# Layer 0 of a hybrid decoder trunk: the product of probabilities and values emitted one step later

## The chip, the cores and the metric

The kernel runs on one core of a Trainium2 chip. The metric is the device time of one execution in microseconds (us); the time of a kernel is the median of its runs. Its engines are named as in the profile: PE (TensorE, matrix products; PEld are its weight loads), DVE (VectorE), ACT (ScalarE), POOL (GpSimd) and SP (SyncE, which issues the transfers).

## The reference, cut to what matters

The input x is [1, 512, 1024] in float32. Two residual layers and a last norm follow one another; the change lies in layer 0:

```python
def even_layer(x, g_norm, w_in, b_f, w_out):
    z = rms_norm(x, g_norm) @ w_in             # [512, 8208]
    qa, ka, va, ga, fa, qb, kb, vb, gb = split(z)
    ya = forgetting_attention(qa, ka, va, log_sigmoid(fa + b_f))   # 16 heads x 64
    yb = dilated_attention(qb, kb, vb)                             # 16 heads x 64
    y = concatenate([ya * silu(ga), yb * silu(gb)])
    return x + y @ w_out
```

Both attentions are causal softmax attentions over 512 tokens. In forgetting attention the logit of query t and key s gets c_t - c_s, with c the running sum of the log forget gates. The dilated one is the mean, weighted by their denominators, of three dilated windows; the kernel folds it into one softmax with an added table. Layer 1 is chunkwise retention with a group norm, a gate and an output projection.

## The kernel before, in words

All matrix products run on numbers split into a high and a low part: `split(hi, lo, src)` rounds on ACT (line 132) and subtracts on DVE (line 134 or 136). A product of two split matrices takes three matmuls (`three`, lines 186 to 188). In the profile the line numbers of these helpers stand for many users, so the names of the tiles tell them apart: `pf` and `pt` are projections, `po` the output projection, `w_h` and `w_l` the split weights, `ka` and `kl` the high and low part of projected keys, `pth` and `ptl` those of the transposed probabilities, `yh` and `yl` those of the gated output.

The 32 heads of layer 0 go in 8 groups of 4, in the order dilated, four forgetting, three dilated. In stage n the attention of group n is emitted in 16 steps (4 heads times k = 0 to 3), and between the steps, in equal shares, the fillers: the gate projection of group n, the value projection of group n + 1, the output projection of an earlier group, and the key and query projections of group n + 1. The function `interleave` does that.

A step (hn, k) works on three heads at once. For head hn it emits the scores and the softmax of query block 3 - k (PE lines 442 and 443, DVE `pi` line 446, ACT exp line 448, DVE reciprocal line 449, POOL scaling line 450). For head hn - 1 it emits the transposes of key block k (PE line 457) and their split into `pth` (ACT) and `ptl` (DVE). Then come the products of the probabilities and values (`pv_block`): two matmuls per key block, with `pth` (line 469) and with `ptl` (line 470), summed up in the PSUM tile `ps_o`. After key block 3 `finish_head` reads `ps_o`: ACT copies one half to `tmp` (line 483), DVE adds the other to give `y` (line 484); after every second head POOL multiplies by the gate (line 486), and ACT and DVE split the result into `yh` and `yl`.

Buffers that the text comes back to: `ps_o` has one, `pth` and `ptl` have one for each key block, `kl` has one. `kl` and `ka` are the source of three transfers that SP issues (lines 396 to 398), so that the next `kl` can be written only after these have read the last:

```python
                kl = qp.tile([P, S], F32R, tag="kl", name="kl", bufs=1)
                split(ka, kl, ps)
                dma(out=r32(kb[64:128, :]), in_=r32(kl[64:128, :]))
                dma(out=r32(kb[0:64, :]), in_=r32(ka[64:128, :]))
                dma(out=r32(ka[64:128, :]), in_=r32(kl[0:64, :]))
```

A group's key projection gives two such `kl` (heads 0 and 1, heads 2 and 3).

What each engine executes in which order is not the order of emission itself: except in a part at the start that asks for its own order, the framework that builds the program orders the instructions of each engine, earlier emission first where several are ready by its own estimate of times. On the chip each engine then takes its list as it stands.

Of the kernel before, what the change touches and what calls it, by code (L numbers as in the profile page):

```python
# [14 lines left out]
P = 128  # L15
# [5 lines left out]
WARM = 12                     # matmuls that raise the tensor engine's clock  # L21
# layer 0: the order of the groups of 4 heads, dilated (D) and forgetting (F), and
# the groups whose output projection runs beside the attention of a group
# [3 lines left out]
OFF = (0, 128, 384, 768)      # column of query block i in a packed lower triangle  # L27
OFFT = (0, 512, 896, 1152)    # column of key block j in a packed transposed triangle
# [3 lines left out]
def _tables():  # L32
    """Constants that depend on the shapes alone."""
    p = np.arange(P)[:, None]
    g = np.arange(S)[None, :]
    ident = np.eye(P, dtype=np.float32)

    d = p - g + 384
    mult = ((d >= 0) & (d <= 128)).astype(np.int64)
    mult += (d >= 0) & (d % 4 == 0)  # L40
    mult += (d >= 0) & (d % 16 == 0)
    dil = np.where(mult > 0, -np.log(np.maximum(mult, 1).astype(np.float64)), MASKED).astype(np.float32)

    causal = np.where(np.arange(P)[None, :] <= p, 0.0, MASKED).astype(np.float32)

    half = 128
    inv = (np.float32(1.0) / (np.float32(10000.0) ** np.linspace(0.0, 1.0, half, dtype=np.float32))).astype(np.float32)
    ang = (np.arange(S, dtype=np.float32)[None, :] * inv[:, None]).astype(np.float32)
    rot = np.stack([np.cos(ang.astype(np.float64)), np.sin(ang.astype(np.float64))], axis=1).astype(np.float32)

    lg = np.log1p(-np.power(np.float32(2.0), np.float32(-5.0) - np.arange(4, dtype=np.float32))).astype(np.float32)
    rel = (g - p).astype(np.float64)
    dec = np.where(rel[:, None, :] >= 0,
                   np.exp(lg.astype(np.float64)[None, :, None] * np.maximum(rel, 0.0)[:, None, :]),
                   0.0) / 16.0
    return {"ident": ident, "dil": dil, "causal": causal, "rot": rot, "dec": dec.astype(np.float32)}
# [3 lines left out]
def trunk(ctx: ExitStack, tc, x, even_norm, even_w_in, even_b_f, even_w_out,  # L60
# [17 lines left out]
    xres = keep.tile([P, NT, D], F32, name="xres")  # L78
    xT = keep.tile([P, 2, KT, S], F32R, name="xT")     # normed x^T: high part, low part
# [4 lines left out]
    # the table of the first square roots, loaded beside the first transfers  # L84
# [9 lines left out]
    def rstd_of(v):  # L94
        """1 / sqrt(v) of a [128, 1] tile, refined by a Newton step."""
        sd = sm.tile([P, 1], F32, tag="sd", name="sd")
        act.activation(sd, v, AF.Sqrt)
        r = sm.tile([P, 1], F32, tag="rs", name="rs")
        dve.reciprocal(r, sd)
        e = sm.tile([P, 1], F32, tag="re", name="re")  # L100
        dve.scalar_tensor_tensor(e, r, v, r, ALU.mult, ALU.mult)
        dve.tensor_scalar(e, e, -0.5, 1.5, ALU.mult, ALU.add)
        dve.tensor_tensor(r, r, e, ALU.mult)
        return r

    def row_scale(t, junk):
        """1 / rms of the rows of token tile t of the residual; junk: a tile to write the squares to."""
        ss = sm.tile([P, 1], F32, tag="ss", name="ss")
        act.activation(junk, xres[:, t, :], AF.Square, accum_out=ss)
        v = sm.tile([P, 1], F32, tag="var", name="var")  # L110
        dve.tensor_scalar(v, ss, 1.0 / D, EPS, ALU.mult, ALU.add)
        return rstd_of(v)
# [3 lines left out]
    def half_stats(st, t, c, junk):  # L116
        """The same, from the two halves of the columns; the second gives 1 / rms."""
        ss = sm.tile([P, 1], F32, tag="ss", name="ss")
        act.activation(junk, xres[:, t, c * H:(c + 1) * H], AF.Square, accum_out=ss)
        v = sm.tile([P, 1], F32, tag="var", name="var")  # L120
        dve.tensor_scalar(v, ss, 1.0 / D, st["v"] if c else EPS, ALU.mult, ALU.add)
        st["v"] = v
        if c:
            st["r"] = rstd_of(v)

    def rms(t, gain, dst):
        """dst = rms_norm of token tile t of the residual."""
        dve.scalar_tensor_tensor(dst, xres[:, t, :], row_scale(t, dst), gain, ALU.mult, ALU.mult)

    def split(hi, lo, src, scale=1.0):  # L130
        """hi + lo = scale * src, each with 12 significant bits."""
        act.activation(hi, src, AF.Copy, scale=scale)  # L132
        if scale == 1.0:
            dve.tensor_tensor(lo, src, r32(hi), ALU.subtract)  # L134
        else:
            dve.scalar_tensor_tensor(lo, src, scale, r32(hi), ALU.mult, ALU.subtract)
# [11 lines left out]
    # a chunk is (DRAM [rows, cols], deinterleave); rows * cols = 512 * 256  # L148
# [41 lines left out]
    # Pieces of tensor engine work: a list of chunks and a generator that emits  # L190
    # the work and yields the time of the matmuls emitted since the last yield.
    def proj_features(w, c0, done, deinterleave=False):
        """done(b, PSUM [128 features, 512 tokens]) for the two halves of 256 columns of w."""
# [17 lines left out]
    def proj_tokens(w, c0, done, by_tile=False):  # L211
        """done(b, PSUM [128 tokens, 2 token tiles, 256 columns]) for the two pairs of token tiles.
        by_tile: one token tile after the other, as x^T comes."""
# [21 lines left out]
    def out_proj(y, w, rows, by_tile=None):  # L235
        """residual += y^T^T @ w; a chunk is 256 rows, from rows[i], of 512 columns;
        y(i): the high and low parts of two row tiles of y^T.
        by_tile: all of the weights held, the token tiles finished one after the other."""
        nc_, nk = len(rows), 2 * len(rows)
        # the chunk beyond the buffers of the stream has its own  # L240
# [30 lines left out]
    def interleave(steps, fillers, upto=None):  # L271
        """Emit the steps with the fillers' work between them: evenly, or the share upto[i]
        of it by the end of step i; the rest after the last step."""
# [14 lines left out]
    # =================== layer 0 ===================  # L288
# [17 lines left out]
    with ExitStack() as l0:  # L306
# [7 lines left out]
        bf = cst.tile([32, 1], F32, name="bf")              # for the products with the low part: 0  # L314
# [8 lines left out]
        c_th = cst.tile([P, NT, 16], F32, name="c_th")      # -c, [token, tile, head]  # L323
# [3 lines left out]
        def forget_gates():  # L327
            c_hs = ap_.tile([16, S], F32, tag="bias", name="c_hs", bufs=3)   # [head, token]
# [25 lines left out]
            dve.tensor_tensor(na, zz, nz, ALU.min)          # -|z|  # L354
            e = tl("f_e")
            act.activation(e, na, AF.Exp)                   # exp(-|z|)
            # log1p(e) = 2 atanh(s), s = e / (2 + e) <= 1/3
# [13 lines left out]
            # log_sigmoid = min(z, 0) - 2 pol  # L371
# [17 lines left out]
        def evac_k(store):  # L389
            def done(b, ps):  # L390
# [4 lines left out]
                # both heads [h; l]  # L395
# [6 lines left out]
        def evac_q(store):  # L402
            def done(b, ps):
                # both heads [h; l] and [l; h]
# [11 lines left out]
        def evac_v(store):  # L416
            def done(b, ps):
# [4 lines left out]
                # even heads [vh | vl], odd heads [vl | vh]  # L422
# [14 lines left out]
        def softmax_block(hs, i):  # L437
# [6 lines left out]
            st = sm.tile([P, 3], F32, tag="st", name="st", bufs=8)     # -max, sum, 1/sum  # L444
# [27 lines left out]
        def finish_head(hs):  # L472
            """O = high + low part; after a pair of heads: y = O * silu(g), split."""
# [15 lines left out]
        def fox_bias(head):  # L489
            """(c_s - c_t) and the causal mask, built two blocks ahead of their use."""  # L490
# [60 lines left out]
        order = []          # fillers of stage n, beside the attention of group n  # L551
# [14 lines left out]
        def step(hn, k):  # L566
            """Blocks of the bias two steps ahead, of the softmax of head hn, of P^T and P V of the heads before."""
            def go():
# [8 lines left out]
                if 0 <= hn - 1 < len(heads):  # L577
                    transpose_block(heads[hn - 1], k)
                    if k:
                        pv_block(heads[hn - 1], k - 1)  # L580
                if k == 0 and hn >= 2:
                    pv_block(heads[hn - 2], 3)
                    finish_head(heads[hn - 2])
            return go

        # the tensor engine's clock rises under load: keep it busy while x comes
# [31 lines left out]
        for n in range(8):  # L618
            steps = [step(hn, k) for hn in range(4 * n, 4 * n + 4) for k in range(4)]
            if n == 7:  # L620
                steps += [step(32, k) for k in range(4)] + [step(33, 0)]
# [4 lines left out]
    # =================== layer 1 ===================  # L626
    with ExitStack() as l1:
# [10 lines left out]
        def rotate_done(r, which):  # L638
            """[128 frequencies, 2 parities, 512 tokens], rotated and split."""
# [109 lines left out]
        # the last head: its output projection follows the token tiles  # L749
# [40 lines left out]
```

## Time and profile before

| | us |
|---|---|
| median of 3 runs | 1036.57 |
| lowest and highest run | 1035.21, 1036.67 |
| span of the profiled execution, first to last instruction | 1035.3 |
| PE busy | 1002.6 |
| DVE busy | 637.0 |
| ACT busy | 472.4 |
| POOL busy | 247.4 |

The page of the profile gives a span for the profiled execution and no time of its own beside it; the median of the runs is 1.3 us longer than this span. Busy shares are of the span. In a timeline the first two columns are the start from the span's start and the duration, both in us, and a bracket holds the idle time of the engine before the instruction and what ended it. `L470` is line 470 of the kernel. Ends of matmuls are modelled by the profiler, starts are recorded.

### The profile page before, as it was taken

Reading aid. Unit: us, or ns where it says so; the run is one execution under the profiler, and the core shown is the slowest. Engines: PE = TensorE matmul, PEld = TensorE weight load, DVE = VectorE, ACT = ScalarE, POOL = GpSimd, SP = SyncE. Lnnn points to the kernel's source line nnn. Section 1 sums busy time; section 2 is a strip of 40 time slices with the busy share of each in tenths; the row PEclk is TensorE's granted clock in tenths of the full one; section 3 lists DMA queues with packets and bytes.
Section 4 is the critical chain, followed back from the end, with each engine's and each line's share of the span. In section 5 each row is a group of like instructions: output and inputs, shape, how many; then the busy total and the mean of one; then the engine's idle time right before and its main releaser. Section 6 shows DMA issues by size and latency. Waiting matters only on the chain.

```text
span 1035.3 us, 15756 instructions
## 1 busy us (share of the span) xinstructions
PE 1002.6 (97%) x5836; PEld 869.6 (84%) x5836; DVE 637.0 (62%) x1389; ACT 472.4 (46%) x987; POOL 247.4 (24%) x326
## 2 busy tenths in 40 slices
PE   5999999999999999999999989999999999999997
PEld 5879788888887888987887769978998899889975
DVE  6465676575584576675657684377645744674476
ACT  5345464464554545644657473333323232333233
POOL 3011354454354352211212140023100300030012
PEclk8999999999999999999999999999999999999999
DMA  7554878635647776437454125321222222312112
GB/s 211 133 134 90 150 100 103 177 77 120 156 90 108 143 84 139 107 79 145 76 130 123 41 62 184 102 79 64 82 82 91 72 82 82 102 61 95 69 41 82
DMA packets 84444, 107.42 MB, mean 104 GB/s; under 512 B 6016, under 2 KB 63616, under 8 KB 84240
## 3 DMA queue, kind: packets, MB, share of 16 engines
q1 hardware_dynamic: 84368, 106.42, 43.4%
q8 instruction: 46, 0.75, 0.3%
q14 instruction: 30, 0.25, 0.1%
HBM read 85.39 MB, written 2.13 MB: 85 GB/s over the span
## 4 chain that ended last, share of the span: by engine, by line
PE 81%; DVE 7%; DMA 5%; ACT 4%; issue 2%; POOL 1%; SPq 0%; DVEq 0%; POOLq 0%; ACTq 0%
PE pf L186 10%; PE pf L187 10%; PE pf L188 10%; PE pt L186 8%; PE pt L188 8%; PE pt L187 8%; PE po L186 5%; PE po L188 5%; PE po L187 5%; PE ps_pt L457 3%; DMA kb<-ka 2%; PE ps_o L470 2%; DVE w_l L134 2%; PE ps_o L469 2%; PE ps_s L443 1%
## 5 line engine op out<-in xcount | busy, mean ns | idle before, releaser
L134 DVE TENSOR_TENSOR w_l<-w_raw,w_h 128x512 fp32r<-128x512 f32 x288 | 218.3, 785 | 95.0 <-ACT w_h L132 81.7
L132 ACT ACTIVATE w_h<-w_raw 128x512 fp32r<-128x512 f32 x288 | 169.5, 627 | 186.0 <-PE pf L187 60.2
L186 PE MATMUL pt<-w_h,xT 128*128 128x256 f32 x768 | 217.1, 283 | 2.2 <-ACT xT L132 2.1
L188 PE MATMUL pt<-w_h,xT 128*128 128x256 f32 x768 | 215.7, 281 | 1.6 <-DVE xT L134 1.6
L187 PE MATMUL pt<-w_l,xT 128*128 128x256 f32 x768 | 215.5, 281 | 0.0
L186 PE MATMUL pf<-xT,w_h 128*128 128x512 f32 x512 | 204.4, 399 | 0.0
L188 PE MATMUL pf<-xT,w_l 128*128 128x512 f32 x512 | 202.9, 396 | 0.0
L187 PE MATMUL pf<-xT,w_h 128*128 128x512 f32 x512 | 202.9, 396 | 0.0
L450 POOL TENSOR_SCALAR pi<-pi,st 128x512 f32<-128x512 f32 (+3 forms) x128 | 73.5, 575 | 377.2 <-DVE st L449 346.6
L186 PEld LDWEIGHTS pt<-w_h,xT 128*128 128x128 f32 x768 | 145.3, 189 | 3.7 <-ACT xT L132 2.9
L188 PEld LDWEIGHTS pt<-w_h,xT 128*128 128x128 f32 x768 | 145.2, 189 | 1.8 <-DVE xT L134 1.8
L187 PEld LDWEIGHTS pt<-w_l,xT 128*128 128x128 f32 x768 | 145.2, 189 | 1.1 <-DVE w_l L134 0.2
L188 PEld LDWEIGHTS pf<-xT,w_l 128*128 128x128 f32 x512 | 96.5, 188 | 23.2
L186 PEld LDWEIGHTS pf<-xT,w_h 128*128 128x128 f32 x512 | 96.7, 189 | 19.9
L187 PEld LDWEIGHTS pf<-xT,w_h 128*128 128x128 f32 x512 | 96.7, 189 | 19.6
L132 ACT ACTIVATE pth<-ps_pt 128x512 fp32r<-128x512 f32 (+3 forms) x128 | 55.3, 432 | 98.2 <-PE ps_pt L457 85.7
L448 ACT ACTIVATE pi<-pi,st 128x512 f32<-128x512 f32 (+3 forms) x128 | 71.4, 558 | 44.4 <-DVE st L446 43.8
L704 POOL TENSOR_TENSOR yn<-yn,gate 128x512 f32<-128x512 f32 x16 | 21.9, 1367 | 262.8 <-DVE yn L703 249.4
L253 DVE TENSOR_TENSOR xres<-po,xres 128x512 f32<-128x512 f32 x88 | 59.6, 683 | 26.6 <-PE po L188 26.1
L134 DVE TENSOR_TENSOR ptl<-ps_pt,pth 128x512 fp32r<-128x512 f32 (+3 forms) x128 | 62.2, 487 | 21.2 <-ACT pth L132 19.4
L457 PE MATMUL ps_pt<-ident,pi 128*128 128x128 f32 x320 | 56.8, 275 | 0.1
L446 DVE CUSTOM_DVE_ANT_0 pi<-ps_s,bias 128x512 f32<-128x512 f32 (+1 forms) x64 | 30.8, 487 | 40.6 <-PE ps_pt L457 20.6
(155 smaller groups left out, 1614.1 us busy)
## 6 DMA issues: line engine op xcount, KB each, us to landing
w_raw<-in_even_w_in_dram SPq DMA_DIRECT2D x64, 512.0 KB, 5.6
w_raw<-in_odd_w_in_dram SPq DMA_DIRECT2D x48, 512.0 KB, 3.5
w_raw<-in_even_w_out_dram SPq DMA_DIRECT2D x16, 512.0 KB, 4.3
w_raw<-in_odd_w_out_dram SPq DMA_DIRECT2D x16, 512.0 KB, 3.5
qb<-qa SPq DMA_DIRECT2D x32, 128.0 KB, 2.9
qb<-qa SPq DMA_DIRECT2D x16, 256.0 KB, 3.2
qa<-qa SPq DMA_DIRECT2D x32, 128.0 KB, 3.1
cs<-c_dram SPq DMA_DIRECT2D x16, 256.0 KB, 3.6
```

What stands on the lines that cost most here:

```text
L132: act.activation(hi, src, AF.Copy, scale=scale)
L134: dve.tensor_tensor(lo, src, r32(hi), ALU.subtract)
L186: pe.matmul(ps, lhsT=ah, rhs=bh, start=first, stop=False)
L187: pe.matmul(ps, lhsT=ah, rhs=bl, start=False, stop=False)
L188: pe.matmul(ps, lhsT=al, rhs=bh, start=False, stop=last)
L253: dve.tensor_tensor(xr, ps, xr, ALU.add)
L446: dve.tensor_tensor_reduce(pi[:, 0:n], ps[:, 0:n], hs["bias"](i), 1.0, 3e38, ALU.add, ALU.min, st[:, 0:1])
L448: act.activation(pi[:, 0:n], pi[:, 0:n], AF.Exp, bias=st[:, 0:1], scale=-1.0, accum_out=st[:, 1:2])
L450: pool.tensor_scalar(pi[:, 0:n], pi[:, 0:n], st[:, 2:3], 1.0, ALU.mult, ALU.mult)
L457: pe.transpose(pt[:, (i - j) * P:(i - j + 1) * P], hs["p"][i][:, j * P:(j + 1) * P], ident)
L469: pe.matmul(po[:, j * P:S], lhsT=v, rhs=th[:, 0:n], start=(j == 0), stop=False)
L704: pool.tensor_tensor(yn, yn, r["g"][:, i, :], ALU.mult)
```

## The change

Of a head whose transposes are emitted in steps (hn, 0) to (hn, 3), key block j was multiplied in the step after its transposes; now it is multiplied two steps after. So key blocks 2 and 3 fall into the first two steps of the next head, and `finish_head`, which follows key block 3, is emitted in step k = 1 in place of k = 0. Stage 7 has one step more at its end, 22 in place of 21, over which its fillers are spread.

```diff
                 if 0 <= hn - 1 < len(heads):
                     transpose_block(heads[hn - 1], k)
-                    if k:
-                        pv_block(heads[hn - 1], k - 1)
-                if k == 0 and hn >= 2:
-                    pv_block(heads[hn - 2], 3)
-                    finish_head(heads[hn - 2])
+                    if k >= 2:
+                        pv_block(heads[hn - 1], k - 2)
+                if k < 2 and hn >= 2:
+                    pv_block(heads[hn - 2], k + 2)
+                    if k == 1:
+                        finish_head(heads[hn - 2])
...
             if n == 7:
-                steps += [step(32, k) for k in range(4)] + [step(33, 0)]
+                steps += [step(32, k) for k in range(4)] + [step(33, k) for k in range(2)]
```

The rest of the diff removes comments.

## The prediction

> **What bounds the kernel now.** I read the page first (which engine is busy), then the waits of TensorE, then VectorE's timeline around the waits, then TensorE's.
>
> ```profile
> span 1035.3 us, 15756 instructions
> ...
> PE 1002.6 (97%) x5836; PEld 869.6 (84%) x5836; DVE 637.0 (62%) x1389; ACT 472.4 (46%) x987; POOL 247.4 (24%) x326
> ```
>
> TensorE (PE) is busy for 97% of the span, so whatever the change is worth must come out of the 33 us in which it waits, or add to them. The waits of PE by who ended them (columns: total us, times, longest us), and one line of the same view for VectorE (DVE):
>
> ```profile
> PE ps_o L470 <- DVE ptl L134: 4.1, 4, 2.3
> PE po L186 <- DVE v L134: 0.9, 4, 0.3
> PE ps_o L469 <- ACT pth L132: 0.5, 1, 0.5
> PE ps_o L469 <- DVE y L484: 0.4, 1, 0.4
> ```
>
> ```profile
> DVE kl L134 <- DMA ka<-kl: 11.4, 6, 3.5
> ```
>
> The product of probabilities and values (lines 469 and 470) waits 4.1 us for `ptl`, the low half of the transposed probabilities. Why `ptl` is late shows in DVE's timeline at the longest of these waits, in the stage of group 3 (start, duration; in brackets the idle time before):
>
> ```profile
> 318.35 0.69 DVE L134 TENSOR_TENSOR kl<-pf,ka 128x512 fp32r<-128x512 f32 x1
> ...
> 320.07 0.69 DVE L484 TENSOR_TENSOR y<-ps_o,tmp 64x512 f32<-64x512 f32 x1 [0.36 <-ACT tmp L483]
> ...
> 327.05 0.69 DVE L134 TENSOR_TENSOR kl<-pf,ka 128x512 fp32r<-128x512 f32 x1 [3.52 <-DMA ka<-kl]
> 327.66 0.68 DVE L134 TENSOR_TENSOR w_l<-w_raw,w_h 128x512 fp32r<-128x512 f32 x1
> 328.26 0.55 DVE L446 CUSTOM_DVE_ANT_0 pi<-ps_s,bias 128x384 f32<-128x384 f32 x1
> ...
> 328.73 0.55 DVE L134 TENSOR_TENSOR ptl<-ps_pt,pth 128x384 fp32r<-128x384 f32 x1
> ```
>
> `kl` has one buffer. The second `kl` of a group's key projection must wait until the transfers out of the first have landed, 3.52 us here, and all that is queued behind it on DVE stands still with it. On PE at that place:
>
> ```profile
> 317.93 0.28 PE L470 MATMUL ps_o<-ptl,v 128*128 128x128 f32 x1
> ...
> 322.17 0.48 PE L469 MATMUL ps_o<-pth,v 128*128 128x512 f32 x1
> ...
> 326.58 0.42 PE L469 MATMUL ps_o<-pth,v 128*128 128x384 f32 x1
> 329.34 0.44 PE L470 MATMUL ps_o<-ptl,v 128*128 128x384 f32 x1 [2.33 <-DVE ptl L134]
> ```
>
> These are the products of key blocks 3 (the head before), 0 and 1 in three steps k = 0, 1, 2. The block between k = 1 and k = 2 is where DVE is shut. The clock goes down after the wait:
>
> ```profile
> 330.00:333.50 3.50, 3.50 (x11) 2.68 (x10) 1.81 (x6) 1.75 (x4) 3.33 (x6) 0.51 1.02 90
> ...
> 474.00:477.50 3.50, 3.50 (x15) 2.88 (x16) 2.22 (x7) 2.22 (x7) 1.07 (x2) 1.00 0.91 158
> ```
>
> In the 3.5 us from 330.0 the granted clock is 0.51 (column before the DMA share), so that stretch did about half its work: another 1.7 us lost. After the next longest wait, 1.20 us before 474, the clock stays at 1.00.
>
> **The change part by part.** Only emission order changes: no instruction is added or removed, and the moved step issues no DMA, so SP's queue is passed by nothing. Moved by one step are the two products of a key block (PE), and with the last one finish_head: `tmp` (ACT), `y` (DVE), and after each second head the gate product (POOL), `yh` (ACT), `yl` (DVE). On PE a product passes one step's fillers, two score products and the transposes; on POOL the gate product passes one scaling by 1/sum and two bias instructions, which have room (POOL 24% busy).
>
> *Edit 1, the product one step later.* `ptl` of key block 1 is then wanted a whole step after 326.58, some 4.4 us later (322.17 to 326.58 is one step), so at about 331, and is there at 328.73 + 0.55 = 329.28. All 4.1 us of this wait go, and the 0.5 us for `pth`. The buffers allow it: `pth` and `ptl` of a block have one buffer each, written again four steps after, and the last read moves from one step after to two.
>
> *Edit 2, finish_head one step later.* This is the part that costs. The accumulator `ps_o` has one buffer: the first product of the next head may start only when `y` has read it. Shown at the limit, 0.05 us from the end of `y` (576.26 + 0.70) to the product:
>
> ```profile
> 576.26 0.70 DVE L484 TENSOR_TENSOR y<-ps_o,tmp 64x512 f32<-64x512 f32 x1
> ```
>
> ```profile
> 577.01 0.50 PE L469 MATMUL ps_o<-pth,v 128*128 128x512 f32 x1
> ```
>
> Before, `y` of the head in question ran at 320.07, ahead of the second `kl`, and the next head's product at 322.17 had 1.41 us to spare. Now the last product stands at 322.17, `tmp` follows, and `y` comes to DVE in the very step in which the second `kl` holds it; the next head's first product takes the place at 326.58. What is late next is `y` instead of `ptl`. If DVE keeps its order (`kl`, `w_l`, `pi`, `ptl`) and `y` goes last, `y` starts 0.08 before `ptl` ends (as `ptl` does behind `pi`), and ends at 329.28 - 0.08 + 0.69 = 329.89; the product starts at 329.94. Before, PE went on at 329.34 with the first product of the pair (0.26 undisturbed, below) done; now at 329.94 with none of it: 0.60 + 0.26 = 0.86 us more lost.
>
> The same place comes in every stage that projects keys. The waits at groups 0 and 5 are:
>
> ```profile
> 112.47 0.44 PE L470 MATMUL ps_o<-ptl,v 128*128 128x384 f32 x1 [0.28 <-DVE ptl L134]
> ```
>
> ```profile
> 473.97 0.44 PE L470 MATMUL ps_o<-ptl,v 128*128 128x384 f32 x1 [1.20 <-DVE ptl L134]
> ```
>
> Groups 0, 2, 3 and 5 are the 4 waits of the list. At group 1 the wait is just covered and at group 4 it isn't there:
>
> ```profile
> 183.86 0.42 PE L469 MATMUL ps_o<-pth,v 128*128 128x384 f32 x1
> 184.27 0.44 PE L470 MATMUL ps_o<-ptl,v 128*128 128x384 f32 x1
> ```
>
> ```profile
> 401.70 0.42 PE L469 MATMUL ps_o<-pth,v 128*128 128x384 f32 x1
> 401.96 0.34 PE L470 MATMUL ps_o<-ptl,v 128*128 128x384 f32 x1
> ```
>
> ```profile
> 401.12 0.55 DVE L134 TENSOR_TENSOR ptl<-ps_pt,pth 128x384 fp32r<-128x384 f32 x1
> ```
>
> (0.26 us is the undisturbed distance of the pair, 401.70 to 401.96; group 1's 0.41 holds a wait of 0.15.) Group 4: `ptl` ends at 401.67, `y` would let the product start at 402.33, 0.63 after 401.70. So with `y` last: 5 x 0.86 + 0.63 = +4.9 us in all, on top of the 4.1 us that merely change their name.
>
> The other end: `y` directly behind the second `kl`, at 327.05 + 0.61 + 0.69 + 0.05 = 328.40 instead of 329.94, 1.54 us earlier. Against before that is 0.86 - 1.54 = -0.68 per waiting place, but no more than there is to win: 0.68 at groups 3 and 5, 0.25 and 0.15 at 2 and 1, and 0.1 at group 0, together about -2 us. Between them: the score reduction `pi` moves ahead of the `kl`, because `yl` no longer fills DVE there; `y` is then 0.47 us earlier (328.26 to 328.73) at five places, +2.5 us. The order of each engine is made when the program is built, so the trace of before can't say which; I take the middle of the last two, +3.7, as `y` hangs on `tmp`, which hangs on the last product, and is ready after all the others.
>
> *The clock.* At group 3 PE would wait over 3 us, so the 1.7 us stay. At group 5 the wait becomes 1.2 + 0.86 = 2.1 us, between the 1.20 that didn't lower the clock and the 2.33 that did: 0 to 1.7 us, taken at 0. [...]
>
> *Gains elsewhere.* The 0.5 us for `pth` goes; so should the 0.4 us for `y` (504 us, where ACT's table loads for the gate delay `tmp`; one step later they are past): -0.9 us.
>
> *The output projection.* From the last product (317.93) to the end of `yl` it is 5.6 us:
>
> ```profile
> 322.84 0.69 DVE L134 TENSOR_TENSOR yl<-y,yh 128x512 fp32r<-128x512 f32 x1 [0.15 <-ACT yh L132]
> ```
>
> In the stage of group 1 the last product would stand at about 143.9 (the step's product below), so `yl` is done at 149.5; it is read at 151.24:
>
> ```profile
> 143.75 0.50 PE L469 MATMUL ps_o<-pth,v 128*128 128x512 f32 x1
> ```
>
> ```profile
> 151.24 0.40 PE L188 MATMUL po<-w_h,yl 128*128 128x512 f32 x1
> ```
>
> 1.7 us are left: no cost, and where it fails up to 0.3 us in each of 4 stages, the size of the present waits on `v` behind the same engines (0.9 in 4). The extra step at the end of layer 0 holds the same work before the last output projection: 0.
>
> **Sum**: +3.7 - 0.9 = +2.8 us. The profiled span of 1035.3 becomes 1038.1. The median of the runs, 1036.57, is 1.3 us over the span; taken over unchanged, 1039.4 us.
>
> **Rivals.**
> - *y gets out early* (faster). DVE's order at build time puts `y` directly behind the second `kl`, or ahead of it. For it: `kl` is emitted before, but the order is free. Against: before, `kl` stood ahead of instructions that were ready earlier than `y` will be. Directly behind: -2.0 - 0.9, and -1.7 if the wait of 328.40 - 326.58 = 1.82 us left at group 3 no longer lowers the clock: 1032.0 to 1033.7. If `y` starts before 326.58 - 0.05 - 0.69 = 325.84 there, so ahead of the `kl`, all the waits go: 4.1 + 0.5 + 0.4 + 1.7 = 6.7 us, 1029.9.
> - *The change does nothing*: the wait for `ptl` turns into one for `y` of the same length (`pi` and `w_l` ahead of the `kl`); within 2 us of 1036.57. For it: the same `kl` releases both.
> - *The clock falls at group 5 too*, and the output projection waits: +4.9 - 0.9 + 1.7 + 1.2 = +6.9, 1043.5.
>
> **How the numbers follow.** What can be told from no change is 0.2%, 2 us. `y` queued behind `kl` with the others: 0.60, of which 0.50 above 1038.6 and 0.10 below; nothing: 0.18 (0.02 of it slower); early: 0.22. So slower 0.52, same 0.26, faster 0.22. The likeliest case alone: 1037.5 to 1043.5. With the other signs the range reaches from 1032.5 (the early case without the full gain) to 1043.5.
>
> **What would show it.** Right: PE's wait on `ptl` at L470 is gone, and a wait of L469 <- DVE y takes its place, about 9 us in 5 to 6 waits, at k = 2 behind the second `kl`; the clock still falls near 330. Wrong: L469 <- DVE y stays near 0.4 us, or `y` stands ahead of `kl` in DVE's timeline.

## The result, and the profile after

The changed kernel takes 1051.18 us (median of 4 runs, 1048.15 to 1053.60), the kernel before 1036.62 us beside it: ratio 1.0136, 95% interval 1.0108 to 1.0164. It is slower, as forecast, but by 14.6 us in place of 2.8. The execution that was profiled took 1052.45 us with a span of 1050.6 us:

```profile
span 1050.6 us, 15763 instructions
...
PE 1007.5 (96%) x5836; PEld 873.3 (83%) x5836; DVE 629.2 (60%) x1389; ACT 472.6 (45%) x987; POOL 248.9 (24%) x326
```

The engines have the same numbers of instructions as before. PE's idle time grows by 10.4 us (from 32.7 to 43.1); its busy time grows by 4.9 us at 5836 products in both, 3.0 of it up to the first score product (279 products in both, up to 62.52 us before and 63.95 after), where the granted clock is 0.89 against 0.95. The waits of PE in layer 0 that changed (total us, times, longest us):

```profile
PE ps_o L469 <- DVE y L484: 6.3, 6, 2.6
PE ps_s L442 <- DMA qa<-qa: 6.2, 4, 2.3
...
PE po L186 <- DVE v L134: 3.3, 5, 0.9
...
PE ps_pt L457 <- POOL pi L450: 2.0, 2, 1.8
```

The wait for `ptl` (4.1 us) and that for `pth` are gone and one for `y` stands in their place, as forecast. The other three rows are in no term of the forecast's sum: the scores (L442) wait for the copies of the projected queries, the output projection for the evacuation of `v` (projections and output projection share three PSUM buffers, so it waits for one to be read out), the transposes for POOL's scaling. Before, the second was 0.9 us, the third was not on the list, and the first was

```profile
PE ps_s L442 <- DMA qa<-qa: 1.0, 1, 1.0
```

Where the time goes by stage, from the start of the first score product of each group (row L442 in PE's timeline):

| us | start | 0 | 1 | 2 | 3 | 4 | 5 | 6 | 7 and layer 1 |
|---|---|---|---|---|---|---|---|---|---|
| before | 62.52 | 64.36 | 71.30 | 71.48 | 75.14 | 70.98 | 72.24 | 58.54 | 488.74 |
| after | 63.95 | 65.57 | 72.29 | 72.81 | 76.05 | 72.16 | 75.43 | 61.45 | 490.93 |
| more | 1.43 | 1.21 | 0.99 | 1.33 | 0.91 | 1.18 | 3.19 | 2.91 | 2.19 |

The first 1.43 us are not taken for the change's: nothing of it is emitted there, the clock is lower there (above), and the kernels below start anywhere from 62.2 to 64.2 us, the slower ones and the faster ones alike. The rest comes in every stage, about 1 us in each of stages 0 to 4, some 3 in 5 and in 6, and 2.2 behind, so it is not the one long stall at group 3 on which the prediction dwelt.

What holds the others up shows in the waits of ACT and DVE. Before:

```profile
ACT yh L132 <- POOL y L486: 16.5, 16, 1.5
```

```profile
DVE yl L134 <- ACT yh L132: 3.8, 10, 1.3
```

After:

```profile
ACT yh L132 <- POOL y L486: 40.9, 16, 6.3
```

```profile
DVE yl L134 <- ACT yh L132: 24.6, 13, 2.6
```

These waits are 24 us longer on ACT and 21 us longer on DVE, with the split of the gated output at the head of the engine's list. One place, in the stage of group 2, in the timelines of DVE, POOL and ACT before:

```profile
248.55 0.69 DVE L484 TENSOR_TENSOR y<-ps_o,tmp 64x512 f32<-64x512 f32 x1 [0.36 <-ACT tmp L483]
...
249.33 1.29 POOL L486 TENSOR_TENSOR y<-y,gate 128x512 f32<-128x512 f32 x1 [0.27 <-DVE y L484]
...
250.66 0.63 ACT L132 ACTIVATE yh<-y 128x512 fp32r<-128x512 f32 x1 [0.70 <-POOL y L486]
...
251.32 0.69 DVE L134 TENSOR_TENSOR yl<-y,yh 128x512 fp32r<-128x512 f32 x1 [0.15 <-ACT yh L132]
...
253.45 0.69 DVE L134 TENSOR_TENSOR kl<-pf,ka 128x512 fp32r<-128x512 f32 x1 [1.43 <-DMA ka<-kl]
```

All of it was done 1.4 us before the second `kl`. After, in the order of time:

```profile
257.72 0.69 DVE L134 TENSOR_TENSOR kl<-pf,ka 128x512 fp32r<-128x512 f32 x1 [1.67 <-DMA ka<-kl]
258.33 0.15 DVE L449 RECIPROCAL st<-st 128x1 f32<-128x1 f32 x1
...
258.58 0.58 POOL L450 TENSOR_SCALAR pi<-pi,st 128x384 f32<-128x384 f32 x1 [4.47 <-DVE st L449]
...
258.97 0.69 DVE L484 TENSOR_TENSOR y<-ps_o,tmp 64x512 f32<-64x512 f32 x1
...
259.75 1.29 POOL L486 TENSOR_TENSOR y<-y,gate 128x512 f32<-128x512 f32 x1 [0.58 <-DVE y L484]
...
261.07 0.63 ACT L132 ACTIVATE yh<-y 128x512 fp32r<-128x512 f32 x1 [4.21 <-POOL y L486]
261.61 0.37 ACT L132 ACTIVATE pth<-ps_pt 128x256 fp32r<-128x256 f32 x1
...
261.73 0.69 DVE L134 TENSOR_TENSOR yl<-y,yh 128x512 fp32r<-128x512 f32 x1 [2.07 <-ACT yh L132]
```

The reciprocal waits on DVE behind `kl`, POOL's scaling for the reciprocal, the gate product behind the scaling and for `y`, `yh` for the gate product, `yl` for `yh`. Meanwhile ACT does nothing for 4.21 us and DVE for 2.07, though `pth` behind `yh` could have gone when its transposes were done (PE L457 from 258.85, 0.38 us long), 1.8 us before `yh` began: ACT stayed idle for these 1.8 us and took `yh` first. All that ACT and DVE do next is late, up to the evacuation of the queries 8.36 us after `kl` where it was 7.51 before:

```profile
260.96 0.60 ACT L132 ACTIVATE qa<-pf 128x512 fp32r<-128x512 f32 x1
```

```profile
266.08 0.58 ACT L132 ACTIVATE qa<-pf 128x512 fp32r<-128x512 f32 x1
```

(before, then after). From there to the first score product it is about as long in both (8.70 us to 269.66 before, 8.54 us to 274.62 after): evacuation, copies and their landing, which PE now waits for. PE after, at the starts of groups 3 and 6, and at an output projection:

```profile
274.62 0.65 PE L442 MATMUL ps_s<-ka,qa 128*128 128x512 f32 x2 [0.62 <-DMA qa<-qa]
...
302.30 0.47 PE L186 MATMUL po<-w_h,yh 128*128 128x512 f32 x1 [0.91 <-DVE v L134]
...
498.26 0.64 PE L442 MATMUL ps_s<-ka,qa 128*128 128x512 f32 x2 [2.33 <-DMA qa<-qa]
```

Behind the last of these the granted clock falls to 0.57 (third number from the end), so that some 1.5 of 3.5 us are lost:

```profile
499.00:502.50 3.50, 3.50 (x13) 2.93 (x12) 2.04 (x7) 2.15 (x6) 0.00 (x0) 0.57 0.95 164
```

### The profile page after: what moved, and what is told of

Read it like the earlier page. It is cut to its first block, busy times and chain, and to the rows that moved or that the text cites. A ratio compares the mean times of both kernels' runs of the same rounds, so it can differ in the third digit from the quotient of the medians.

```text
span 1050.6 us, 15763 instructions
## 1 busy us (share of the span) xinstructions
PE 1007.5 (96%) x5836; PEld 873.3 (83%) x5836; DVE 629.2 (60%) x1389; ACT 472.6 (45%) x987; POOL 248.9 (24%) x326
## 4 chain that ended last, share of the span: by engine, by line
PE 75%; DVE 9%; DMA 7%; ACT 5%; issue 2%; POOL 2%; SPq 0%; DVEq 0%; ACTq 0%; POOLq 0%
PE pf L186 9%; PE pf L187 9%; PE pf L188 9%; PE pt L188 7%; PE pt L187 7%; PE pt L186 7%; PE po L186 4%; PE po L188 4%; PE po L187 4%; DVE w_l L134 2%; DMA kb<-ka 2%; PE ps_pt L457 2%; DMA qb<-qa 2%; PE ps_o L469 1%; PE ps_s L442 1%
## 5 line engine op out<-in xcount | busy, mean ns | idle before, releaser
L134 DVE TENSOR_TENSOR w_l<-w_raw,w_h 128x512 fp32r<-128x512 f32 x288 | 211.8, 761 | 98.3 <-ACT w_h L132 93.1
L457 PE MATMUL ps_pt<-ident,pi 128*128 128x128 f32 x320 | 57.1, 276 | 2.5 <-POOL pi L450 2.0
L469 PE MATMUL ps_o<-pth,v 128*128 128x512 f32 (+3 forms) x128 | 50.2, 392 | 6.5 <-DVE y L484 6.3
```

What stands on the lines that cost most here:

```text
L457: pe.transpose(pt[:, (i - j) * P:(i - j + 1) * P], hs["p"][i][:, j * P:(j + 1) * P], ident)
L469: pe.matmul(po[:, j * P:S], lhsT=v, rhs=th[:, 0:n], start=(j == 0), stop=False)
```

## The experiments

Theory A: what costs is finish_head's later place, by the chain just shown. Theory B: the later product itself, with the order that the build makes of it. More rivals came up on the way. C: a weight load that is issued earlier makes the copies of the queries slow. D: a later split costs wherever it stands. E: as soon as the stall of group 3 is gone, the copies of the queries meet a slow weight load. F: the order of SP's list alone makes the copies slow.

### Undoing one half each

finish_head back at its old step, products late:

```diff
                     if k >= 2:
                         pv_block(heads[hn - 1], k - 2)
-                if k < 2 and hn >= 2:
-                    pv_block(heads[hn - 2], k + 2)
-                    if k == 1:
-                        finish_head(heads[hn - 2])
+                if k == 0 and hn >= 2:
+                    pv_block(heads[hn - 2], 2)
+                    pv_block(heads[hn - 2], 3)
+                    finish_head(heads[hn - 2])
...
```

> The products stay one step late (key blocks 0 and 1 at k = 2 and 3, blocks 2 and 3 together at k = 0), but finish_head goes back to the step it had before the change. Theory A (finish_head's later place costs: y and the gate part stand behind the second kl on VectorE and push q's copies, v's evacuation and stage 7's pi back): TensorE's waits for ptl (4.1 us) and for y (6.3 us) are both gone, its wait on qa is back to about 1 us and that on v to about 1 us, the clock does not fall near 335; 1029 to 1033 us. Theory B (the later product itself, with the new order that the build makes of it, costs): still 1044 to 1052 us, with the qa wait near 6 us.

1041.67 us, ratio 1.0061 (1.0046 to 1.0076): between the two theories. The waits for `ptl`, `y` and `v` are as A says (none, none, 1.2 us), but PE waits for `qa` more than ever:

```profile
PE ps_s L442 <- DMA qa<-qa: 10.8, 3, 6.2
```

That is not the chain of theory A; it is taken up below.

finish_head late, products as little as possible:

```diff
-                    if k >= 2:
-                        pv_block(heads[hn - 1], k - 2)
-                if k < 2 and hn >= 2:
-                    pv_block(heads[hn - 2], k + 2)
-                    if k == 1:
-                        finish_head(heads[hn - 2])
+                    if k == 2:
+                        pv_block(heads[hn - 1], 0)
+                    if k == 3:
+                        pv_block(heads[hn - 1], 1)
+                        pv_block(heads[hn - 1], 2)
+                if k == 0 and hn >= 2:
+                    pv_block(heads[hn - 2], 3)
+                if k == 1 and hn >= 2:
+                    finish_head(heads[hn - 2])
```

> The last product of a head is back at its old step (k = 0), blocks 1 and 2 together at k = 3, block 0 at k = 2; only finish_head is one step later than before (k = 1). Theory A: the loss stays, 1043 to 1052 us, with qa waits of 4 us and more and v waits near 3 us, though the waits for y shrink because y's input is a step older. Theory B: the loss goes, 1032 to 1038 us.

1046.26 us, 1.0100 (1.0085 to 1.0115), with 6.7 us of `qa` waits, 4.0 of `v` and only 0.5 of `y`. Two thirds of the loss (10.1 of 14.6 us) stay when PE hardly waits for `y` and the products are near their old places, so B is not the cause of these.

The kernel before with the gate part alone one step later:

```diff
             dve.tensor_tensor(y[stay, :], po[stay, :], tmp[stay, :], ALU.add)
+
+        def gate_pair(hs):
+            g, (pair, e) = hs["g"], divmod(hs["hd"], 2)
             if e == 1:
+                y = g["y"]
                 pool.tensor_tensor(y, y, g["gate"][0][:, pair, :], ALU.mult)
                 split(g["yh"][:, pair, :], g["yl"][:, pair, :], y)
...
+                if k == 1 and hn >= 2:
+                    gate_pair(heads[hn - 2])
...
```

> The kernel before with only the pair's gate part (GpSimd's product, yh, yl) one step later; products, tmp and y stay where they were. If the gate part is what pushes the evacuations back (theory A, second half): TensorE's wait on v rises from 0.9 to about 3.3 us and the wait on POOL's pi in stage 7 appears (about 2 us), 1039 to 1044 us. If y behind kl is what does it: v and pi waits stay as before, 1036 to 1038 us; the ptl wait of 4 us stays in both.

1045.55 us, 1.0099 (1.0082 to 1.0116): the gate part costs by itself as much as the whole of finish_head did in the run above, and more than was expected, for its `qa` waits came too (5.0 us). The `v` wait is 3.6 us as expected; the scaling wait in stage 7 did not come (0.2). `y` is on time here; the product of it is not:

```profile
257.19 0.59 POOL L450 TENSOR_SCALAR pi<-pi,st 128x384 f32<-128x384 f32 x1 [4.79 <-DVE st L449]
257.74 1.30 POOL L490 TENSOR_TENSOR y<-y,gate 128x512 f32<-128x512 f32 x1
```

```profile
ACT yh L132 <- POOL y L490: 44.5, 16, 6.8
```

POOL's scaling holds the gate product back in POOL's list, and so `yh` in ACT's.

The changed kernel with two buffers for `kl` (the forget gates' weights move to other buffers to make room):

```diff
-                kl = qp.tile([P, S], F32R, tag="kl", name="kl", bufs=1)
+                kl = qp.tile([P, S], F32R, tag="kl", name="kl", bufs=2)
...
```

> The changed kernel with two buffers for kl, so that the second kl no longer waits for the transfers out of the first (room for it comes from placing the forget gates' weights in buffers that are free at that time). Theory A: the block on VectorE is what finish_head's later place runs into, so the waits for y (6.3 us) and most of those on qa (6.2 us) go, the clock stays up; 1030 to 1036 us. Rival C (the earlier w_raw load makes q's copies slow by itself): the qa wait stays at 4 us or more and the time above 1041 us.

1040.59 us, 1.0045 (1.0031 to 1.0060). The `y` wait goes (0.4 us), but ACT still waits 30.9 us for the gate product, and the `qa` wait is 7.7 us with 3.6 in one piece; from 300 to 375 us, where PE is idle for 4.1 us, the granted clock is 0.98 on average, in the 75 us behind it 1.00. Without the block by `kl` 10.6 of the 14.6 us are gone (the kernel before wins 1.7 by the same edit, below). The time stays above the 1036 us that was expected because of the `qa` wait, as rival C had it; what makes these copies slow is found below.

### The place of the split

The kernel before with yh and yl alone one step later, the gate product at its old place:

```diff
             if e == 1:
                 pool.tensor_tensor(y, y, g["gate"][0][:, pair, :], ALU.mult)
-                split(g["yh"][:, pair, :], g["yl"][:, pair, :], y)
+
+        def split_y(hs):
+            g, (pair, e) = hs["g"], divmod(hs["hd"], 2)
+            if e == 1:
+                split(g["yh"][:, pair, :], g["yl"][:, pair, :], g["y"])
...
+                if k == 1 and hn >= 2:
+                    split_y(heads[hn - 2])
...
```

> The kernel before with only the split of the gated y (yh on ScalarE, yl on VectorE) one step later; GpSimd's gate product stays at its old step, ahead of the second kl. Theory A, made sharper by the gate-part run (there ScalarE sits 44 us idle at the head of its queue with yh, because GpSimd's product is queued behind a scaling by 1/sum that waits for the reciprocal behind the second kl): here the product is done before ScalarE comes to yh, so ScalarE's wait for POOL's y is under 8 us, the qa wait about 1 us, the v wait at most 2 us; 1035 to 1038 us. Rival D (any later yh and yl cost, by the place that they take on ScalarE and VectorE): as the gate-part run, 1042 to 1047 us.

1033.87 us, 0.9976 (0.9965 to 0.9986): faster than before, where the run with the gate product late as well was 9 us slower. POOL has the product done ahead of the scaling, and ACT waits less than in the kernel before (16.5 us):

```profile
249.91 1.29 POOL L486 TENSOR_TENSOR y<-y,gate 128x512 f32<-128x512 f32 x1 [0.27 <-DVE y L484]
```

```profile
ACT yh L132 <- POOL y L486: 11.8, 10, 1.5
```

So the later split by itself cost nothing (rival D falls); in the gate part late, where ACT meets the split up to 6.8 us before POOL is done, 9.4 us were lost. The sum of ACT's waits is no price by itself. The four slowest kernels (the changed one, finish_head alone late, the gate part late, and the one that follows here) each have a single hold of 6.2 to 6.9 us; the fastest of all (early finish_head with other columns, below) has a larger sum than the kernel before, in holds of 2.6 us at most:

```profile
ACT yh L132 <- POOL y L486: 26.0, 16, 2.6
```

The changed kernel with the split (taken out of finish_head as above) at k = 2:

```diff
                     if k == 1:
                         finish_head(heads[hn - 2])
+                if k == 2 and hn >= 2:
+                    split_y(heads[hn - 2])
...
```

> The changed kernel with yh and yl one further step later (k = 2), y and GpSimd's product where the change put them. Theory A: ScalarE's wait for POOL's y falls from 41 us to under 12, the v wait from 3.3 to under 1.5 us, the qa wait from 6.2 to 2 to 4 us (the stage of group 5 may keep its own); TensorE's waits for y stay near 6 us; 1040 to 1046 us. Rival D: later is worse, 1050 us and more.

1046.83 us, 1.0099 (1.0082 to 1.0117). It tells little: the build put `yh` at nearly the same place in ACT's list, the wait for POOL is still 38.2 us in 15, and stages 0 to 4 are as long as in the changed kernel within 0.2 us each. What is won lies at the start (1.7 us, where the change does nothing) and from stage 5 on, where the wait for POOL's scaling is 0.8 us in place of 2.0.

The changed kernel with the split on GpSimd:

```diff
-                split(g["yh"][:, pair, :], g["yl"][:, pair, :], y)
+                pool.tensor_copy(g["yh"][:, pair, :], y)
+                pool.tensor_tensor(g["yl"][:, pair, :], y, r32(g["yh"][:, pair, :]), ALU.subtract)
```

> The changed kernel with yh and yl made on GpSimd, behind its gate product, in place of ScalarE and VectorE: nothing that waits for GpSimd stands in the queues of ScalarE and VectorE any more, while product and finish_head stay where the change put them. Theory A: TensorE's v wait falls from 3.3 to about 1 us, the qa wait from 6.2 to 1 to 4 us; the y waits (6 us) stay; 1038 to 1045 us, less what GpSimd's longer work (some 2 us for each pair) adds to the scalings by 1/sum. Rival (y behind kl on VectorE alone makes the loss): 1047 us and more.

1036.75 us, 1.0009 (0.9998 to 1.0019): level with the kernel before, and lower than expected. Nothing of ACT or DVE waits for POOL's product any more, the `v` wait is off PE's list, and of `qa` one wait is left:

```profile
PE ps_o L469 <- DVE y L484: 4.9, 7, 2.4
...
PE ps_pt L457 <- POOL pi L450: 3.6, 3, 2.2
...
PE ps_s L442 <- DMA qa<-qa: 1.6, 1, 1.6
```

The control, the same two lines in the kernel before:

> Control for the changed kernel with yh and yl on GpSimd: the same move in the kernel before. If yh and yl in the queues of ScalarE and VectorE cost nothing before the change (TensorE shows no wait that goes back to them), this comes out at 1034 to 1038 us, and the whole 14 us between the changed kernel and its version with the split on GpSimd are the change's loss through that queue. If the move helps by itself, it comes out at 1029 to 1033 us, and what is left between it and the 1036.8 us of the changed kernel with the split on GpSimd is what the rest of the change costs: the turn from y to the accumulator, forecast at +3.7 us, and GpSimd's late scalings in stage 7.

1032.71 us, 0.9958 (0.9943 to 0.9974). The move helps by itself by 4 us. It wins 14.4 us in the changed kernel and 4.1 in the kernel before, so some 10 of the 14.6 us of the loss went through `yh` and `yl` in the lists of ACT and DVE, and 4.0 us (1036.75 less 1032.71; 4.9 when each is set against the kernel before beside it) are left for all the rest of the change. The profiled spans of the two differ by 2.0 us (1033.6 and 1031.6): 1.5 less up to the start of stage 7 and 3.5 more from there on, with POOL's late scalings in stage 7 (3.6 us of wait; none in the control). In the control stands, for the turn by `y`:

```profile
PE ps_o L470 <- DVE ptl L134: 3.8, 4, 1.9
```

So 4.9 us of waits for `y` stand against 3.8 for `ptl` and 0.6 for `y` in the control: the turn from `y` to the accumulator costs 0.5 us more than what it replaced, or 1.1 if the 0.6 are not counted.

### The copies of the queries

Why did the early finish_head wait 6.2 us for `qa`? SP in that run, at the end of the stage of group 3:

```profile
333.39 0.54 SPq L155 DMA_DIRECT2D w_raw<-in_even_w_in_dram  x1
336.13 0.37 SPq L155 DMA_DIRECT2D w_raw<-in_even_w_out_dram  x1
337.35 0.47 SPq L410 DMA_DIRECT2D qb<-qa  x1
...
347.36 0.46 SPq L411 DMA_DIRECT2D qa<-qa  x1
```

The copies are issued 4 us behind one weight load and 1.2 us behind another, and the copy of line 411, which waits for those before it, comes 10 us later: the first copies take 8.2 to 8.8 us to land here (medians), where those at the same place of the kernel before, from 336 us on, take 2.6 to 3.1. Loads have no equal times: in the kernel before, the 6 from 131 us on (group of index 1), then the 6 from 203 us on (group of index 2), KB and median us to landing:

```profile
w_raw<-in_even_w_in_dram SPq DMA_DIRECT2D x6, 512.0 KB, 7.7
```

```profile
w_raw<-in_even_w_in_dram SPq DMA_DIRECT2D x6, 512.0 KB, 5.3
```

The loads that stand ahead of the copies at the ends of stages 0 and 3 are those of index 1. Theory E: whatever lets PE pass group 3's stall brings the copies into this load. In the changed kernel itself, of the `qa` waits only the one at group 1 (1.55 us, 1.04 before) has such loads ahead of it; those at groups 6 and 7 (2.33 and 1.69 us) do not.

The kernel before with two buffers for `kl` (the same line as above):

> The kernel before with two buffers for kl (same room as in the changed kernel with two). If the block on VectorE is all that the ptl wait is: that wait (4.1 us) goes and the clock stays up near 333 us; without any new wait 1030 to 1032 us. Theory E (whatever takes group 3's wait away brings q's copies close behind the slow weight load of that stage, which takes over 8 us): a qa wait of 3 to 6 us comes in the stage of group 3, and the time is 1033 to 1037 us.

1035.22 us, 0.9986 (0.9973 to 0.9998). The `ptl` wait is gone, and at the end of that stage stands

```profile
343.83 0.67 PE L442 MATMUL ps_s<-ka,qa 128*128 128x512 f32 x2 [3.93 <-DMA qa<-qa]
```

The stall moved by 14 us and grew, as E has it; in all, 1.7 us are won.

Early finish_head, with one load of each q projection held until the copies are out:

```diff
-                h, l = weights()
+                h, l = weights(load=not (hold and kc == 1))
...
                             done(b, ps[b])
+                            if hold and b == 1:
+                                load_next()
```

> The kernel with the product later and finish_head at its old step, and the second weight load that is issued during each q projection held until q's copies are issued. Theory E: the copies share the DMA engines with one load in place of two, so the qa waits fall from 10.8 us to under 6 us (the 6.2 us at 350 to under 4), 1034 to 1038 us; if the held loads then come late, ScalarE waits for w_raw instead, and TensorE for w_h. Rival: the qa waits stay at 10 us, the loads are not what the copies wait for, 1040 to 1043 us.

1042.17 us, 1.0062 (1.0033 to 1.0092), `qa` waits 10.2 us. It settles nothing: the load held was the one at 349.63, and the two ahead of the copies (333.20 and 335.83) went out as before: they belong to the two uses of `weights()` ahead of the one that the edit changes.

Early finish_head, index 1 reading the columns of index 2:

```diff
-                base, ... = [4112 + 1024 * i + 256 * j for i in range(4)], ...
+                base, ... = [4112 + 1024 * i + 256 * (j if j != 1 else 2) for i in range(4)], ...
...
```

Two of the eight groups then work with the weights of two others, so this kernel does not compute the layer; the work is of the same size.

> The kernel with the product later and finish_head at its old step, whose groups of index 1 read the weights of the columns of index 2 in place of their own (same sizes, other columns: the results of these groups are of other weights). In all traces so far the loads of the groups of index 1 take 7.4 to 9 us from issue to landing, of other groups 4.7 to 6.4 us. Theory E (q's copies at the ends of stages 0 and 3 lie behind such a slow load): these loads now take 4.7 to 6.4 us, the qa waits of 3.9 and 6.2 us shrink to under 1.5 us each, the clock stays up after them, 1029 to 1034 us. Rival F (the copies are slow by the order of SyncE's queue alone): the qa waits stay above 8 us, 1040 us and more.

1027.77 us, 0.9916 (0.9901 to 0.9932), lower than expected. The load that took 9.5 us takes 4.8, and the `qa` waits are down from 10.8 to 0.3 us (early finish_head, then this kernel, the load ahead of the copies):

```profile
w_raw<-in_even_w_in_dram SPq DMA_DIRECT2D x1, 512.0 KB, 9.5
```

```profile
w_raw<-in_even_w_in_dram SPq DMA_DIRECT2D x1, 512.0 KB, 4.8
```

Stages 1 to 5 are now 71.05 to 71.26 us each, with PE idle for 0.3 us in each: no stall is left in them. The 13.9 us between the two kernels are the slow loads, since only the addresses read differ, and rival F (SP's order) falls.

The control, the kernel before with the same columns:

> Control: the kernel before with the same exchange of columns. Its q copies meet the slow loads only in the stage of group 0 (1.0 us of qa wait), so by theory E little is to be won: 1034.5 to 1037 us, with the loads at 4.7 to 6.4 us. If the slow loads cost the kernel before more than that wait, it comes out below 1034 us.

1032.49 us, 0.9966 (0.9956 to 0.9976), 2 us lower than expected: the stage of group 3 goes from 75.14 to 71.32 us. The stall with which the prediction begins was itself the slow load, in which the copies out of `kl` stood:

```profile
DVE kl L134 <- DMA ka<-kl: 7.8, 5, 2.3
```

```profile
PE ps_o L470 <- DVE ptl L134: 1.4, 2, 1.2
```

(11.4 and 4.1 us before.) With slow loads out of the way on both sides, the late product with an early finish_head wins 4.7 us (1032.49 less 1027.77). Of these 1.4 are the waits for `ptl` that it takes away (those for `pth` stay, 0.8 us for 0.5); where the rest comes from is open.

### Versions meant to beat both

The kernel before with the product late but for groups 0 and 3, finish_head at its old step, and the split one step later or on GpSimd:

```diff
+                    late_pv = (hn - 1) // 4 not in (0, 3)
+                    if late_pv and k >= 2:
+                        pv_block(heads[hn - 1], k - 2)
+                    if not late_pv and k:
+                        pv_block(heads[hn - 1], k - 1)
...
```

> A version meant to beat both: finish_head at its old step, yh and yl one step later (1033.9 us by itself), and the product later only for heads of the groups whose stage does not run into the slow load (all but groups 0 and 3). The waits for ptl at groups 1, 2 and 5 (about 1.7 us) go, those at groups 0 and 3 stay, qa waits stay near 1 us: 1031 to 1033.5 us. If the product's later place has a cost of its own, 1034 us and more.

1032.34 us, 0.9955 (0.9937 to 0.9974).

> A version meant to beat both: finish_head at its old step, yh and yl on GpSimd, the product later for all groups but 0 and 3. The ptl waits of groups 1, 2 and 5 go; no ScalarE wait for POOL's y is left; 1029 to 1034 us. If GpSimd's longer work delays the scalings by 1/sum in stage 7 (2 us of it in the changed kernel with the split on GpSimd), 1034 to 1036 us.

1031.82 us, 0.9947 (0.9929 to 0.9965). Both beat both kernels, the second by 5.0 us (1036.78 for the kernel before beside it). The second is not told apart from the control with the split on GpSimd alone (1032.71), so what the late product adds there is open.

## Why the prediction was wrong

- *Edit 1*: right. The waits for `ptl` and `pth` went (4.6 us), and where neither a late finish_head nor a slow load comes in, the late product is a gain (1032.49 to 1027.77).
- *Edit 2, the turn from y to ps_o*: right in kind, too large. Forecast were 9 us of waits for `y` and +3.7; measured 6.3 us, and 0.5 to 1.1 us more than what it replaced in the pair of kernels with the split on GpSimd. On DVE `pi` and `w_l` both moved ahead of `kl`, so that at group 3 only a reciprocal and `ptl` stood between it and `y`, better than the middle that was taken:

```profile
332.95 0.69 DVE L134 TENSOR_TENSOR kl<-pf,ka 128x512 fp32r<-128x512 f32 x1 [3.73 <-DMA ka<-kl]
333.56 0.15 DVE L449 RECIPROCAL st<-st 128x1 f32<-128x1 f32 x1
333.63 0.54 DVE L134 TENSOR_TENSOR ptl<-ps_pt,pth 128x384 fp32r<-128x384 f32 x1
334.20 0.69 DVE L484 TENSOR_TENSOR y<-ps_o,tmp 64x512 f32<-64x512 f32 x1
```

  The place, k = 2 behind the second `kl`, and the fall of the clock near 336 us (0.52 in the 3.5 us from 335.50) were as said.
- *The step that failed* is the sentence that on POOL the gate product "passes one scaling by 1/sum and two bias instructions, which have room (POOL 24% busy)". POOL had the room, but its list has an order: the scaling waits for a reciprocal behind the second `kl`, the product for the scaling, and `yh` and `yl` hold ACT and DVE until it is done (4.47 us of waiting on POOL, 4.21 on ACT and 2.07 on DVE in the place shown). Priced at nothing, this is some 10 of the 14.6 us by the kernels with the split on GpSimd. The same chain cut at its start, with two buffers for `kl`, gives 10.6, or 8.9 beyond what the same edit gives the kernel before. The prediction looked at who waits for `ps_o`, not at who stands behind `yh`.
- *The output projection*, "no cost", or up to 0.3 in 4 stages: its margin was worked out for its own inputs `yh` and `yl`, and it waited no longer for them (0.4 us once, at the end of layer 0, in both kernels). It waited for the evacuation of `v`, late by the same held lists: 3.3 us against 0.9. With the split on GpSimd this wait is gone.
- *The copies of q* were in no term: 6.2 us against 1.0, and a fall of the clock at 499 us (to 0.57).
- *The clock at group 5*, taken at 0, the author's choice between two measured waits (1.20 and 2.33 us): right for the wait on `y` (1.64 us, at 481.7; the clock is 1.00 in the 3.5 us from 483.40), and no guard against the one 17 us later (2.33 us, 0.57).
- *The extra step, 0*: stage 7 and what follows take 2.19 us more, 1.8 of it one wait for POOL's scaling, at 600 us. The step itself is not the reason: the kernel with the split alone late has it too and takes 487.46 us from there, less than the kernel before.
- *The rivals*: "the change does nothing" described the wait for `y` best (6.3 us for 4.6); the third, with waits at the output projection, had the right direction with too few places.

## What to carry to other kernels

When a step is moved, go through every list in which it stands and ask what is behind it there and what it will wait for at the new place; the busy share of the engine said nothing on this here (POOL 24% before and after). The split that waited for POOL did better on POOL (14.4 us less in the changed kernel, 4.1 in the kernel before), or so late that its input was there: with only `yh` and `yl` late, and not the product that they wait for, a loss of 9.4 us became a gain of 3.0. And when a stall is taken away, look what the next transfer meets at its earlier time: in the kernel before, with two buffers for `kl`, a slow load (9.8 us) made the same stall again, and longer (3.93 us for 2.33), 14 us later.

## What the runs showed of the hardware

From 23 us on, a 512 KB load of projection weights takes 7.4 to 8.9 us for the groups of index 1 (16 loads; columns 256 to 511 of each 1024 of either kind) and 4.7 to 6.6 for the others (44 loads) in the kernel before, 7.4 to 9.0 and 4.7 to 6.9 in the changed one. The one ahead of the copies at the end of stage 3 took 9.5 us in the early finish_head and 9.8 in the kernel before with two buffers for `kl`. With the columns of index 2 it took 4.8, and the 6 loads from 131 us on took 5.0 (median), where they take 7.7 in the kernel before. Why is open.

Idle time of PE did not decide by its length alone whether the clock falls. A wait of 2.33 us lowered it in the kernel before (to 0.51 in the 3.5 us from 330.00) and in the changed one (to 0.57 in those from 499.00); one of 2.63 (gate part late) did not (1.00 in those from 494.60), nor did one of 2.41 (split on GpSimd):

```profile
327.11 0.50 PE L469 MATMUL ps_o<-pth,v 128*128 128x512 f32 x1 [2.41 <-DVE y L484]
```

```profile
329.00:332.50 3.50, 3.50 (x19) 2.95 (x18) 2.52 (x5) 1.90 (x5) 3.34 (x4) 1.00 0.78 137
```

Behind other single waits in layer 0 the granted clock was 0.50 (6.2 us, early finish_head, from 350.00), 0.52 (2.56 us, the changed kernel, from 335.50) and 0.55 (2.46 us, the split alone late, from 329.00), and 1.00 behind one of 1.64 us (the changed kernel, from 483.40) and one of 1.20 us (the kernel before, from 474.00). It fell at shorter waits too: at the end of layer 0, about waits of 1.5 and 1.6 us that lie 5 us apart, in the kernel before (0.53 in the 3.5 us from 613.50) and in the changed one (0.74 from 627.50). With waits of 1.4 to 1.5 and of 1.6 us for the same tiles, it is 1.00 from 600 to 650 us in finish_head alone late, in the gate part late and in the changed kernel with two buffers for `kl`. What else decides is open.
